# Sharing a causal attention block over four cores by contiguous pieces, with a program branch per piece

## The chip, the cores and the metric

One Trainium2 chip (trn2), one program on its 8 cores. Cores 0 to 3 form one die and work on the first sequence of the batch, cores 4 to 7 the other die and the second sequence. The metric is device time in microseconds (us) of the slowest core. Executions come in two states: in the fast one all cores have a like granted clock; in the slow one a die runs at a lower clock and is over 1% longer.

Engines in the profile: PE (matmul), PEld (its weight loads, beside PE), DVE (vector), ACT (activation functions), POOL, SP; the last two here mainly issue DMA.

## The reference, cut to what matters

```python
D_MODEL, BATCH, SEQ, N_META = 2048, 2, 4096, 16      # L = 4112 tokens per sequence
ATTN_HEADS, HEAD_DIM, D_FF = 8, 128, 8192

xn = rms_norm(h, norm_mix)
q, k, v, fg, cb, cc, cx, gl = split(xn @ w_in)        # 1024, 1024, 1024, 8, 3 x 1024, 4096 columns
q, k = rms_norm per head of 128
log_f = log_sigmoid(fg + b_fgate)                     # forget gate per token and head
s = q.k / sqrt(128) + cumsum(log_f)[query] - cumsum(log_f)[key];  s = -inf where key > query
a = softmax(s) @ v @ w_attn_out
c = (cb * causal_conv3(cc * cx)) @ w_conv_out
h = h + (sigmoid(gl_a) * a + sigmoid(gl_c) * c) @ w_o
h = h + relu(rms_norm(h, norm_mlp) @ w_up) ** 2 @ w_down
return h[:, N_META:]
```

Inputs and output are float32; both kernels multiply in bf16 with sums in float32. Causality is what the change is about: a query needs only keys before it, so late tokens cost more attention than early ones.

## The kernel before: the parts that the change touches

Every core ran the same instruction stream. Its own 1024 queries were every fourth 128-token block, so each core had to project K and V for all 4112 tokens, in groups of 512:

```python
groups = [(0, 1, NMETA)] + [(NMETA + 512 * g, 4, 128) for g in range(8)]
# ... per group g and head: one diagonal block of queries, then all later ones in threes
trips = [(gi - 1, 1, True)]
r = gi
while r < NR:                                     # NR = 8 query blocks
    n = min(3, NR - r)
    trips.append((r, n, False)); r += n
# ... exp, then a multiply by a mask that differs per core (data, not code)
S.op("act", lambda e: e.activation(out=PTf[:bt, pi, 0:W], in_=sbank[:bt, 0:W], func=AF.Exp,
                                   bias=bias_t[...], scale=SCALE), ...)
if diag:
    S.op("dve", lambda e: e.tensor_tensor(out=PTf[:, pi, 0:128], in0=PTf[:, pi, 0:128],
                                          in1=tri_bf[:, j, :], op=ALU.mult), ...)
```

x was squared on DVE for the token norm, and each head of K went through a norm of its own:

```python
S.op("dve", ... sq = stage * stage); S.op("dve", ... xg = stage * g_mix)          # per 128 rows of x
S.op("pe",  ... pb[sb_][:, :T] += ones_bf.T @ sq)                                 # 512-column sum
# head norm of Q and K: scale, square, 512-column sum, copy, Ln, Exp, final multiply
return [lambda: sA(0), lambda: sA(1), NOP, sB1, sB2, sC1, NOP, sC1b, sC2, sD]
```

Between attention and the rest stood a barrier and a second reading of the core's own x; weights were read straight from their matrices:

```python
S.barrier()
for t in range(2):
    rms_prep(xoT[:, TS[t]], 512, xog[:, :, TS[t]], ...)
# ... (cut)
src_ = dram[row0:row0 + kc * 128, col0:col0 + ncol].rearrange("(kc p) n -> p kc n", p=128)
S.dma("pool", view, src_, writes=keys)            # rows of ncol elements
```

## Time and profile before

The median of the first four runs was 2668.22 us (2665.5 to 2671.61).

The prediction below shows the spans of the cores, the head of the page, its slices, the stretches and PE's waits. One more view matters, the page's list of DMA queues; the queue that carries the weights (packets, MB, share of the 16 DMA engines over the span):

```profile
q0 software_dynamic: 324304, 125.87, 42.0%
```

### The profile page before, as it was taken

The page shows a single profiled execution, that of the slowest core. Times are in us where ns is not written, and L with a number is a line of the kernel's source. Part 1 is how long each engine was busy: PE and PEld are TensorE (multiplying, and loading weights), DVE is VectorE, ACT ScalarE, POOL GpSimd, SP SyncE. Part 2 cuts the span into 40 slices and gives each one's busy share as a digit, 9 for nine tenths or more (in the row PEclk, how much of TensorE's full clock was granted, in tenths as well). Part 3 has the DMA queues.
Part 4 walks back from the last instruction along what each step waited for, and adds up shares of the span by engine and source line. Part 5 has one row for each costly group of instructions (what it writes and reads, how often), then busy time and mean ns, then how long its engine had stood idle before and what let it go on. Part 6 is the DMA issues. An engine that isn't in the chain of part 4 may idle for free.

```text
span 2666.8 us, 36382 instructions; the slowest of 8 cores (2652.6 to 2666.8 us)
## 1 busy us (share of the span) xinstructions
PE 2419.1 (91%) x12522; PEld 1172.0 (44%) x12742; DVE 1027.7 (39%) x2170; ACT 586.9 (22%) x1198; POOL 189.8 (7%) x177
## 2 busy tenths in 40 slices
PE   5678889898988988389999999999999999999999
PEld 1234455554544445034444444444444444444444
DVE  5655546545465455335423233332111211211211
ACT  0312345444443334300011111121001101100100
POOL 1000000000000000111111121000000000000000
PEclk9868889898987968589999999999999999999999
DMA  9930101202022010967578778975566656666662
GB/s 199 127 88 11 54 19 46 64 1 64 1 64 64 1 40 1 184 78 74 58 69 79 72 71 94 162 100 74 76 79 80 79 71 74 77 80 79 78 118 90
DMA packets 366243, 196.12 MB, mean 74 GB/s; under 512 B 161136, under 2 KB 333168, under 8 KB 366064
## 3 DMA queue, kind: packets, MB, share of 16 engines
q0 software_dynamic: 324304, 125.87, 42.0%
q1 hardware_dynamic: 41760, 67.90, 8.8%
q8 instruction: 107, 1.75, 0.3%
q14 instruction: 72, 0.59, 0.1%
HBM read 311.22 MB, written 8.39 MB: 120 GB/s over the span
## 4 chain that ended last, share of the span: by engine, by line
PE 85%; DVE 6%; DMA 4%; issue 3%; ACT 1%; DVEq 0%; another core or an unknown queue 0%; SPq 0%; ACTq 0%
PE pc L875 16%; PE pc L894 16%; PE pb L339 10%; PE pb L434 8%; PE pc L759 6%; PE pc L807 4%; PE pc L805 4%; PE pc L837 4%; DMA stage<-xoT 3%; PE pb L584 3%; PE pb L559 3%; PE pc L803 2%; PE pc L801 2%; PE pb L313 1%; DVE xg L306 1%
## 5 line engine op out<-in xcount | busy, mean ns | idle before, releaser
L875 PE MATMUL pc<-xog,wring 128*128 128x512 bf16 x2008 | 440.6, 379 | 2.1
L894 PE MATMUL pc<-mT,wring 128*128 128x512 bf16 x2006 | 440.5, 379 | 2.2
L568 ACT ACTIVATE PT<-pb,small 128x128 bf16<-128x128 f32 (+4 forms) x664 | 276.4, 454 | 407.1 <-PE pb L559 209.2
L894 PEld LDWEIGHTS pc<-mT,wring 128*128 128x128 bf16 x2048 | 200.4, 98 | 241.6
L875 PEld LDWEIGHTS pc<-xog,wring 128*128 128x128 bf16 x2048 | 200.3, 98 | 241.5
L339 PE MATMUL pb<-xg,wk 128*128 128x512 bf16 (+1 forms) x1123 | 253.0, 369 | 2.6 <-issue 1.0
L434 PE MATMUL pb<-wv,xg 128*128 128x512 bf16 (+1 forms) x1028 | 245.1, 382 | 1.4
L882 ACT ACTIVATE mT<-tmp 128x512 bf16<-128x512 f32 x128 | 80.6, 629 | 691.2 <-DVE tmp L879 691.2
L559 PE MATMUL pb<-QT,KT 128*128 128x128 bf16 (+4 forms) x664 | 190.4, 298 | 46.4 <-ACT PT L568 39.1
L879 DVE SCALAR_TENSOR_TENSOR tmp<-pc,rstd_o 128x512 f32<-128x512 f32 x128 | 88.6, 692 | 355.0 <-PE pc L875 351.2
L898 DVE TENSOR_TENSOR h<-h,pc 128x512 f32<-128x512 f32 x128 | 88.1, 688 | 353.4 <-PE pc L894 353.4
L584 PE MATMUL pb<-Vg,PT 128*128 128x129 bf16 (+1 forms) x1216 | 190.8, 245 | 30.0 <-DVE PT L573 27.4
L759 PE MATMUL pc<-xog,wring 128*128 128x512 bf16 x752 | 166.7, 382 | 1.2 <-issue 0.2
L584 PEld LDWEIGHTS pb<-Vg,PT 128*128 128x128 bf16 (+1 forms) x1216 | 113.3, 108 | 112.4 <-issue 77.7
L112 POOL DMA_DIRECT2D wring<-w_in x56 | 64.3, 1159 | 1370.6 <-issue 964.7
L339 PEld LDWEIGHTS pb<-xg,wk 128*128 128x128 bf16 x1152 | 104.8, 102 | 108.6 <-issue 13.9
L434 PEld LDWEIGHTS pb<-wv,xg 128*128 128x128 bf16 (+1 forms) x1056 | 99.1, 98 | 102.4 <-issue 2.5
L600 DVE SCALAR_TENSOR_TENSOR acc<-acc,small,pb 128x387 f32<-128x387 f32 (+2 forms) x160 | 72.8, 455 | 174.5 <-PE pb L584 160.7
L313 PE MATMUL pb<-sq,ones_bf 128*128 128x512 bf16 (+1 forms) x162 | 82.0, 507 | 62.0 <-DVE sq L304 56.1
L814 DVE TENSOR_TENSOR tmpA<-pc,rstd_o 128x512 f32<-128x512 f32 x64 | 41.3, 686 | 212.1 <-PE pc L807 212.1
L304 DVE TENSOR_TENSOR sq<-stage 128x512 bf16<-128x512 f32 (+1 forms) x176 | 112.7, 640 | 23.4 <-DMA stage<-xoT 11.2
L837 PE MATMUL pc<-mT,wring 128*128 128x512 bf16 x501 | 114.8, 379 | 1.0 <-DVE mT L822 0.5
(116 smaller groups left out, 2135.0 us busy)
## 6 DMA issues: line engine op xcount, KB each, us to landing
stage<-xT SPq DMA_DIRECT2D x128, 256.0 KB, 3.3
wring<-w_up POOLq DMA_DIRECT2D x32, 1024.0 KB, 11.1
wring<-w_down POOLq DMA_DIRECT2D x32, 1024.0 KB, 8.9
wring<-w_in POOLq DMA_DIRECT2D x56, 512.0 KB, 8.8
stage<-xoT SPq DMA_DIRECT2D x96, 256.0 KB, 8.1
wv<-w_in POOLq DMA_DIRECT2D x8, 1024.0 KB, 18.2
wring<-w_o POOLq DMA_DIRECT2D x8, 1024.0 KB, 13.3
yT<-h SPq DMA_DIRECT2D x32, 256.0 KB, 2.0
```

The lines of the kernel that those rows point to most:

```text
L304: S.op("dve", lambda e: e.tensor_tensor(out=sq[:, qi, :T], in0=stage[:, si, :T], in1=stage[:, si, :T], op=ALU.mult), reads=[sk], writes=[qk])
L313: S.op("pe", lambda e: e.matmul(pb[sb_][:, :T], lhsT=ones_bf[:], rhs=sq[:, qi, :T], start=(kc == 0), stop=(kc == KC - 1)), reads=[qk, "one ...
L339: ins = e.matmul(bank[:, :T], lhsT=wbuf[:, kc, h * 128:(h + 1) * 128], rhs=xg[:, kc, :T], start=(kc == 0), stop=(kc == KC - 1))
L434: ins = e.matmul(bank[:bt, :], lhsT=xg[:, kc, j * bt:(j + 1) * bt], rhs=wv[:, kc, ch * 512:(ch + 1) * 512], start=(kc == 0), stop=(kc == K ...
L559: S.op("pe", lambda e: e.matmul(sbank[:bt, 0:W], lhsT=KT[:, h, j * bt:(j + 1) * bt], rhs=QT[:, h, r0 * 128:r0 * 128 + W], start=True, stop ...
L568: S.op("act", lambda e: e.activation(out=PTf[:bt, pi, 0:W], in_=sbank[:bt, 0:W], func=AF.Exp, bias=bias_t[:bt, j * 8 + h:j * 8 + h + 1], s ...
L584: ins = e.matmul(obank[:, k * 129:(k + 1) * 129], lhsT=PTf[:bt, pi, k * 128:(k + 1) * 128], rhs=Vg[:bt, j, h, :], start=(j == 0 and k == 0 ...
L759: ins = e.matmul(bank[:, :], lhsT=w[:, kc, cs], rhs=xog[:, kc, TS[t]], start=(kc == 0), stop=(kc == KC - 1))
L805: ins = e.matmul(pc[b0 + 2][:, :], lhsT=wg0[:, kc, cs], rhs=xog[:, kc, TS[t]], start=(kc == 0), stop=(kc == KC - 1))
L837: ins = e.matmul(pc[bank][:, :], lhsT=wo[:, kc, cs], rhs=mT[:, kc, TS[t]], start=(kc == 0), stop=(kc == KC - 1))
L875: ins = e.matmul(pc[bank][:, :], lhsT=wu[:, kc, cs], rhs=hng[:, kc, TS[t]], start=(kc == 0), stop=(kc == KC - 1))
L894: ins = e.matmul(pc[bank][:, :], lhsT=wd[:, kc, cs], rhs=uT[:, kc, TS[t]], start=(kc == 0), stop=(kc == KC - 1))
```

## The change

The intent: do no arithmetic that causality makes useless, and keep PE fed. Core p of a sequence owns one contiguous piece. The pieces are cut so that the sum of matmul columns is about equal: the late ones have fewer tokens, since they do more attention. As the cores now do different things, the program holds four bodies and each core jumps to its own. With it come smaller changes: x stays on chip (no barrier, no re-reading), K is not normalised but its scale is given to exp, the diagonal mask is added by a matmul, the token squares of earlier tokens are made on ACT with an accumulated sum, and weights are laid out in memory as the tiles that are loaded. The core of a diff of 2303 lines, cuts marked:

```diff
+CUTS = [0, 1200, 2246, 3226, L]
+class Geo:
+    def __init__(self, p):
+        self.A, self.B = CUTS[p], CUTS[p + 1]
+        ...
+        self.et = [(max(0, self.A - 128 * (i + 1)), self.A - 128 * i) for i in range(nt)]   # earlier tokens
+        self.egroups = [list(range(g, min(g + 2, nt))) for g in range(0, nt, 2)]             # 256 at a time
 ...
+    cid = nc.values_load(T["cid"][0:1, 0:1], ...)
+    for p in nc.Switch(engines=engines, index=[cid] * 5, n=4):
+        emit(nc, sems, T, ps, Geo(p))
 ...  K: copy, square, one-column sums per tile of 128 keys; the scale goes into exp
+                S.op("dve", lambda e: e.tensor_copy(out=KT[ks][:, 0:N], in_=ps[st["b"]][:, 0:N]), ...)
+                S.op("dve", lambda e: e.tensor_tensor(out=sqk[sq][:, 0:N], in0=KT..., in1=KT..., op=ALU.mult), ...)
+                    for j, m, off in tiles:
+                        ins = e.matmul(ps[7][:m, col:col + 1], lhsT=sqk[st["q"]][:, off:off + m], rhs=on_h[:, 0:1], ...)
 ...
-                                out=PTf[...], in_=sbank[:bt, 0:W], func=AF.Exp, bias=bias_t[...], scale=SCALE),
-                                if diag: ... tensor_tensor(..., in1=tri_bf[:, j, :], op=ALU.mult)
+                            if diag:
+                                ins = e.matmul(ps[sb][:m, 0:mq], lhsT=id_bf[:, :m], rhs=mask_bf[:, off:off + mq], start=False, stop=True)
+                        S.op("act", lambda e: e.activation(out=PT[pt][:m, 0:N], in_=ps[st["s"]][:m, 0:N], func=AF.Exp,
+                                                           bias=small[:m, bcol:bcol + 1], scale=small[:m, kcol:kcol + 1]), ...)
 ...  token squares of earlier tokens, from a row-major copy of x
+                S.op("act", lambda e: e.activation(out=stage[i][:m, 0:1024], in_=stage[i][:m, 0:1024], func=AF.Square,
+                                                   accum_out=small[:m, col:col + 1]), ...)
 ...  attention steps and the next group's projections laid into one another by their cost
+        th = attn_thunks(units)            # steps of one group, values matmul 3 and accumulation 4 steps after the scores
+        merge(th, fill)                    # fill: V and K of the next group; in the last group some of the convolution
-        S.barrier()
-        ... rms_prep(xoT[:, TS[t]], 512, xog[:, :, TS[t]], ...)
+        S.dma("pool", ringv[i][:, :], T["wB"][k], writes=[("ring", i)])    # one 128 x 2048 tile, ring of eight
```

## The prediction

> **What bounds the kernel now.** I read the list of cores first, because a change that shares the work out anew is decided by the slowest core. The eight spans lie within 14.2 us (2652.6 to 2666.8) at granted clocks of 0.924 to 0.927, so today every core does the same work and none is disturbed. Next the head of the page and its slices:
>
> ```profile
> span 2666.8 us, 36382 instructions; the slowest of 8 cores (2652.6 to 2666.8 us)
> PE 2419.1 (91%) x12522; PEld 1172.0 (44%) x12742; DVE 1027.7 (39%) x2170; ACT 586.9 (22%) x1198; POOL 189.8 (7%) x177
> PE   5678889898988988389999999999999999999999
> PEclk9868889898987968589999999999999999999999
> ```
>
> PE is busy 91%, but the slices show two kernels: up to slice 16 PE has holes and a clock below full; after that it is full at full clock. I cut the span at the barrier and at the changes of source line (table of stretches; columns: us, busy us and instructions per engine, clock, DMA share, GB/s):
>
> ```profile
> 0.00:110.00 110.00, 69.36 (x255) 26.69 (x261) 66.49 (x117) 18.68 (x27) 13.04 (x15) 0.95 1.14 169
> 110.00:232.00 122.00, 94.06 (x523) 41.47 (x529) 68.65 (x168) 30.34 (x62) 2.28 (x2) 0.79 0.39 74
> 232.00:1064.00 832.00, 725.10 (x4544) 405.60 (x4609) 450.86 (x1140) 348.35 (x794) 0.00 (x0) 0.85 0.12 35
> 1064.00:1150.00 86.00, 27.78 (x112) 9.39 (x115) 28.79 (x75) 31.68 (x70) 11.42 (x10) 0.50 1.13 175
> 1784.00:2666.00 882.00, 875.30 (x3994) 398.53 (x4073) 175.94 (x255) 80.50 (x128) 67.34 (x59) 1.00 0.59 81
> ```
>
> Stage A (0 to 1064 us) is Q, then K and V of all 4112 tokens with attention. The next 86 us re-read x behind a barrier at half clock. Stage B (1150 to 2667) is convolution, gates, output projection and MLP: in its last 882 us, 4073 weight loads, so 216.5 ns per 512-column matmul. Stage B is nothing but streamed columns. Where stage A loses time, PE's waits say:
>
> ```profile
> PE pb L313 <- DVE sq L304: 56.1, 60, 8.3
> PE pc L217 <- ACT sq L215: 50.6, 43, 4.8
> PE pb L559 <- ACT PT L568: 39.1, 29, 4.6
> PE pb L584 <- DVE PT L573: 27.4, 42, 2.0
> PE pb L357 <- DVE scr L362: 19.5, 21, 2.9
> ```
>
> The token sums of squares wait for squaring (first, and second for the re-read), the scores for exp, the values matmul for the mask multiply on DVE, the head norms for a copy. One K/V period shows it as well: 650 to 716 us has PE 64.47 of 66 us at clock 1.00; 716 to 760 only 30.98 of 44 at 0.70, while DVE is busy 4.0 of 4.0 us in pieces of it, preparing the next x. So DVE and ordering bound the seams of stage A, PE everything else.
>
> **What the Trainium skill says.** "TensorE: Matmul & The Clock Gate", section "Wait — 56ns, not 53.3ns?": a warm matmul costs N/2.4 ns plus about 2.5. That gives 215.8 for N=512; the trace's 216.5 agrees. The same page's Part 1 (the HAM clock gate) says an idle window of about 3.4 us halves the clock; the 0.50 in the re-read and the 0.70 at the seams agree. It also warns of a 13/16 clock once three cores of a die run dense matmuls; this trace does not show it (1.00 through the MLP on all-core load), so I budget full clock. "DMA: Bandwidth & Descriptors", "Why small descriptors are slow": fixed cost per packet. The weight queue here moved 125.87 MB in 324304 packets, 388 bytes each, at 42% of the engines.
>
> **The change part by part.** I count columns streamed through PE and price them at N/2.4 + 2.5 ns.
>
> *Before.* Stage A: Q 131k columns, x and head norms 123k, K 526k, V 541k, scores 156k, values 157k: 1.634M, 681 us. Stage B with the re-read: 3.572M, 1488 us. Together 2169 us; 2667 were taken. The 498 us above it are 31 of 2.5 ns per matmul (12742 loads), 79 of the re-read (86 less 7 of columns), 19 at stage B's boundaries, and 369 of stage A's seams, small matmuls and half clock (1064 - 681 - 14).
>
> *Removed arithmetic.* Before, a core owned every fourth block, so it projected K and V for the whole sequence and swept masked blocks: 36 x 4 pairs and a meta block per head. Now core p of a batch owns one contiguous piece (cuts 0, 1200, 2246, 3226, 4112) and runs its own branch of the program: it projects K and V only for tokens up to its end, and touches only pairs on or below the diagonal. Pairs per head become 55, 135, 180, 210. The cuts give the late pieces fewer own tokens (n = 1184, 1046, 980, 886), so stage B shrinks or grows with n/1024. Per core, in us at 2.4 columns per ns:
> stage A 257, 430, 567, 684; stage B 1713, 1513, 1418, 1282; sums 1970, 1943, 1985, 1966. With 2.5 ns per matmul (p0: about 12500 matmuls, 31 us; p2 and p3: some 12000 to 13400, 30 to 33; p1 14500, 36): 2001, 1979, 2015, 1999. The saving over 2169 + 31 is 185 us for the worst core, p2.
>
> *Removed overhead.* (1) The x tile stays on chip from Q to the merge, so the barrier and re-read (86 us, of which the 7 us of columns are counted) go: -79. (2) K needs no normalised copy: its per-token scale goes into exp's scale, and its sum of squares is a one-column matmul, so the 512-column norms, copy, Ln, Exp and final multiply per head go. (3) The diagonal mask is a 128-column matmul, in place of 256 multiplies of 222 ns (55.0 us of DVE on PE's path for 27.4). (4) Token squares of earlier tokens go to ACT with an accumulated sum, from a second row-major read of x. (5) The forget-gate sums use pairs of tiles, two fp32 matmuls per 256 keys in place of 14 per 512; with the row-scale ones these were 64 us of PE busy here. (2) to (5) are what should shrink the 369 us, and what replaces them is priced next.
>
> *Does another engine become the bound?* An early group of 256 keys on p2: PE 98k columns, 40.8 us, plus small matmuls, about 43. ACT: per tile and head exp of 384, 384 and 212 columns, 579 + 579 + about 430 ns by the rows measured here, times 16 is 25.4 us; squares about 4 x 1.1, small ones 3: 33 us. DVE: K copies and squares 6, V 4.5, accumulators 8 x 1.6 = 13, scaling x 4.3, small 2: 30 us. PE still bounds, but ACT is 77% full, so I take 5% of the 450 us of p2's mixed part as lost: +22.
>
> *Other terms.* Start: Q's first chunk needs 4.2 MB of weights and 4.0 MB of x. The trace moved 199 GB/s in its first slice: 41 us, 23 of them covered by PE work, then a gap of a few us before the second chunk: +22. First K after V: +4. Boundaries of the MLP quarters and of stages, as stage B had (1517 against 1499): +15. Output tail +2. Core p2: 2015 + 22 + 22 + 4 + 15 + 2 = 2080. Core p3 likewise 1999 + 29 + 43 = 2071. Core p0, whose small own attention is ACT-bound (224 exps of about 0.5 us = 112 against 100 of PE), about 2070.
>
> **The rivals.** *Balance fails.* The cuts equalise columns, not losses: if mixed attention loses 12% rather than 5%, p3 and p2 carry it (580 and 450 us of it) and the kernel ends at 2112 (15%: 2130), with p0 some 40 us earlier. For it: exp rows of 0.37 to 0.58 us and PE waiting 39.1 us for them; against: the stretch 650 to 716, where K/V filled PE to 98%. *Weight traffic becomes the bound.* Each core now streams 2048-column tiles at 16 x 886/2.4 = 5.9 us each, ring of eight; today 1 MB takes a share of 0.59 with a period of 13.8 us. Per tile that is 0.5 MB in 5.9 us, 85 GB/s against 81: share 0.62 at the old packets, less at larger ones. Hidden, I think; the output projection, with three residual buffers at 8.1 us landing and units of 2.4 to 3.4 us, could stall by 10 to 30 us. *Only the removed arithmetic counts:* if seams persist in other places, -185 gives about 2480. The new seams must be far worse than I see for that. *Power:* denser PE on every core could draw the lower clock the page warns of; 13/16 through p2's stage A would add 567 x 3/13 = 131 us, half of that ends at 2145.
>
> **Range and chances.** The rival losses are one-sided: 2080 with a tail to 2130; a start at faster DMA and better overlap gives 2040. Time 2080 us, 2035 to 2135 eight times in ten. For within 2% (above 2615) some 500 us of new loss would be needed. Faster 0.97, same 0.02, slower 0.01.
>
> **What would show it.** Cores: spans within about 2% of each other, p0 (cores 0 and 4) with a stage A near 350 us and p3 with one near 780. No stretch at clock 0.50 after the start; mean clock 0.97 or above. Rows for convolution, gates and MLP at N/2.4 + 2.5 ns of about 396, 350, 490 and 444 columns. PE waits for exp and DVE in the mixed part together below 60 us, and none for weights beyond the start. The prediction is wrong if PE in the attention part is busy under 90%, if one slice is over 3% longer than the rest, or if PE waits on weight tiles in the MLP.

## The result, and the profile after

The median of the ten timed runs is 2208.2 us (2150.87 to 2552.58), against 2668.43 us of before in the same rounds. Ratios in this text are the mean time of one kernel's fast runs over that of the other's of the same rounds, so not quite the ratio of medians: here 0.8069, with a 95% interval of 0.8059 to 0.8078. The direction was right, the size was not: 2080 us was predicted and 2135 us was the top of the range.

Two different things lie in the 2208. Five of the ten timed runs were slow, and their times reach from 2261.25 to 2552.58; the five fast ones lie between 2150.87 and 2155.15, and the median fell between the two sets (2155.15 and 2261.25). A slow run's record shows what that is. Cores 0 to 7 of the one of 2539.29 us, span and clock:

```
2535.3 2536.0 2523.1 2519.6 | 2127.2 2136.8 2142.4 2151.1
 0.811  0.811  0.822  0.822 |  0.992  0.990  0.992  0.990
```

One die lost nearly a fifth of its clock; the other one did its usual time. Of the 14 runs of before three were slow too (2837.67, 2923.95, 3066.34). So what follows is about the fast runs: some 2152 us, 72 more than predicted.

The list of cores (span, mean granted clock) of the profiled run, which was fast:

```profile
core 0: 2129.9 us, clock 0.993
...
core 5: 2145.2 us, clock 0.986
...
core 7: 2148.9 us, clock 0.990
```

The shortest core is 0.9% below the longest: four different programs end together, at almost full clock. The head of the page and its slices:

```profile
span 2148.9 us, 38630 instructions; the slowest of 8 cores (2129.9 to 2148.9 us)
PE 2066.8 (96%) x13886; PEld 1252.5 (58%) x13886; DVE 815.1 (38%) x1920; ACT 682.8 (32%) x1390; POOL 124.4 (6%) x245
PE   4799899999999998999999999999999999999999
PEclk9899999999999999999999999999999999999999
```

The holes and the clock of 5 to 8 tenths that the first sixteen slices of before had are gone but for the first slices. What is left I read from the table of stretches of core 7, the slowest (us; busy us and instructions of PE, PEld, DVE, ACT, POOL; clock; DMA share; GB/s):

```profile
10.00:50.00 40.00, 19.96 (x86) 8.75 (x87) 6.49 (x15) 7.81 (x8) 4.72 (x9) 0.96 1.01 204
50.00:116.00 66.00, 51.01 (x236) 25.51 (x235) 27.30 (x52) 36.77 (x61) 4.58 (x15) 0.87 0.81 169
116.00:167.00 51.00, 51.00 (x340) 34.95 (x339) 15.05 (x47) 0.00 (x0) 0.00 (x0) 0.97 0.28 50
167.00:290.00 123.00, 109.12 (x1141) 89.60 (x1139) 62.83 (x204) 74.38 (x179) 0.00 (x0) 0.97 0.18 54
290.00:805.00 515.00, 504.65 (x4918) 404.45 (x4919) 319.93 (x910) 393.25 (x844) 4.23 (x8) 1.00 0.33 98
805.00:863.00 58.00, 50.83 (x301) 25.14 (x299) 24.77 (x51) 26.44 (x52) 1.59 (x3) 0.91 0.30 57
...
1378.00:2148.00 770.00, 767.43 (x4097) 395.67 (x4096) 158.35 (x256) 76.58 (x133) 63.87 (x121) 1.00 0.53 93
```

A busy share does not tell how much was streamed, because a short matmul's record lasts longer than the gap to the next one (a one-column matmul's record is 165 ns). So I priced the matmuls of each stretch as the prediction did, N/2.4 + 2.5 ns for N columns, the one-column sums at 30 ns and the float32 sums at some 77 ns, as two experiments below give, and took this from the wall time (the stretch left out above, 863 to 1378 us, had PE busy for 512.84 of 515 us):

| core 7, us | wall | streamed | lost | the prediction's loss |
|---|---|---|---|---|
| 0 to 116: Q | 116 | 59 | 57 | 22 (start) |
| 116 to 167: own V | 51 | 49 | 2 | 0 |
| 167 to 290: own K, diagonal groups | 123 | 99 | 24 | 4 (first K) and 29 (5%) for these three |
| 290 to 805: earlier groups | 515 | 495 | 20 | |
| 805 to 863: last group | 58 | 37 | 21 | |
| 863 to 2149: convolution to MLP | 1286 | 1279 | 7 | 17 (boundaries, tail) |
| sum | 2149 | 2018 | 131 | 72 |

The prediction had 1999 streamed and 72 lost for this core, 2071 in all. PE's waits, to set beside those of before:

```profile
PE ps L520 <- DMA v_wq<-wqkv: 28.6, 5, 20.9
PE ps L943 <- ACT v_PT L958: 14.8, 23, 2.8
PE ps L547 <- ACT v_qsq L543: 11.4, 6, 3.3
PE ps L972 <- DVE v_acc L998: 9.3, 15, 2.5
```

The 50 to 56 us waits for squares are gone. Two of the sums of now lie in the start: Q's matmuls wait for Q's weights (28.6 us, of it 20.9 before the first), and the head norms' sums for a square (11.4). The waits for exp and for the accumulator (the two lines shown make 24 us) lie in the attention. Two pieces of the chain that ended last (start us, us, what), and the queue of the weights:

```profile
9.29 11.31 DMA v_wq<-wqkv
...
1474.18 95.89 PE ps L1319 x512
```

```profile
q0 software_dynamic: 33696, 125.94, 34.7%
```

The chain begins with a transfer of 11.31 us and its MLP is blocks of 512 matmuls in 95.9 us, 187.3 ns each at 442 and 444 columns; the priced 443/2.4 + 2.5 is 187.1. The weight queue moves the same bytes in a tenth of the packets (3738 bytes each).

The start in detail. The timeline of core 7 from 66 us (start us, us, engine, line, operation; in brackets the idle time before and what ended it). L547 is the sum of squares of one head on PE, L543 the square on ACT, L551 the Ln of the head norm, whose Exp follows it on ACT; between them DVE scales the next head out of its bank:

```profile
66.55 0.56 ACT L543 ACTIVATE v_qsq<-v_qraw 128x444 bf16<-128x444 f32 x1
...
67.25 0.35 PE L547 MATMUL ps<-v_qsq,v_on_h 128*128 128x444 bf16 x1 [3.32 <-ACT v_qsq L543]
...
67.80 0.63 ACT L551 ACTIVATE v_qrn<-ps,v_cst 128x444 f32<-128x444 f32 x1 [0.70 <-PE ps L547]
...
69.01 0.56 ACT L543 ACTIVATE v_qsq<-v_qraw 128x444 bf16<-128x444 f32 x1
```

From one ACT square to the next head's pass 2.46 us (66.55 to 69.01), and PE has one matmul of 0.35 us in it. Six heads of the first chunk of 444 tokens had been collected in six banks, so for a while there is nothing else for PE: it waits for a chain that goes round PE, ACT and DVE once per head.

### The profile page after: what moved, and what is told of

It is laid out like the page before. It is cut to its first block, busy times and chain, and to the rows that moved or that the text cites. A ratio compares the mean times of both kernels' runs of the same rounds, so it can differ in the third digit from the quotient of the medians.

```text
span 2148.9 us, 38630 instructions; the slowest of 8 cores (2129.9 to 2148.9 us)
## 1 busy us (share of the span) xinstructions
PE 2066.8 (96%) x13886; PEld 1252.5 (58%) x13886; DVE 815.1 (38%) x1920; ACT 682.8 (32%) x1390; POOL 124.4 (6%) x245
## 3 DMA queue, kind: packets, MB, share of 16 engines
q1 hardware_dynamic: 26784, 76.64, 11.5%
## 4 chain that ended last, share of the span: by engine, by line
PE 91%; ACT 3%; DMA 2%; issue 2%; DVE 1%; ACTq 0%; POOLq 0%; DVEq 0%; SPq 0%
PE ps L1299 18%; PE ps L1319 18%; PE ps L660 10%; PE ps L627 10%; PE ps L1204 9%; PE ps L1038 7%; PE ps L1255 4%; PE ps L972 4%; PE ps L943 4%; PE ps L1198 2%; PE ps L1200 2%; DMA v_wq<-wqkv 2%; PE ps L520 2%; ACT v_PT L958 1%; ACT v_stage L878 1%
## 5 line engine op out<-in xcount | busy, mean ns | idle before, releaser
L958 ACT ACTIVATE v_PT<-ps,v_small 128x118 bf16<-128x118 f32 (+4 forms) x752 | 400.8, 584 | 149.9 <-PE ps L943 90.7
L1319 PE MATMUL ps<-v_uT,v_ring 128*128 128x444 bf16 (+1 forms) x2048 | 384.2, 349 | 0.0
L1299 PE MATMUL ps<-v_hng,v_ring 128*128 128x444 bf16 (+1 forms) x2048 | 384.2, 349 | 0.0
L1319 PEld LDWEIGHTS ps<-v_uT,v_ring 128*128 128x128 bf16 x2048 | 197.9, 97 | 185.7
L1299 PEld LDWEIGHTS ps<-v_hng,v_ring 128*128 128x128 bf16 x2048 | 197.8, 97 | 185.7
L943 PE MATMUL ps<-v_QT,v_KT 128*128 128x118 bf16 (+4 forms) x752 | 207.0, 285 | 15.9 <-ACT v_PT L958 14.8
L627 PE MATMUL ps<-v_wv,v_xg 128*128 128x387 bf16 (+3 forms) x1248 | 209.5, 312 | 0.0
L660 PE MATMUL ps<-v_xg,v_wk 128*128 128x256 bf16 (+1 forms) x1664 | 208.4, 269 | 0.0
L972 PE MATMUL ps<-v_VB,v_PT 128*128 128x129 bf16 (+3 forms) x1536 | 185.0, 222 | 13.7 <-DVE v_acc L998 9.3
L1204 PE MATMUL ps<-v_xog,v_ring 128*128 128x442 bf16 (+1 forms) x1024 | 196.8, 350 | 0.0
```

What stands on the lines that cost most here:

```text
L627: ins = e.matmul(ps[b][:m, 0:nh * 129], lhsT=lhs(kc), rhs=wv[:, kc, h0 * 129:(h0 + nh) * 129], start=(kc == 0), stop=(kc == KC - 1))
L660: ins = e.matmul(ps[b][:, 0:N], lhsT=wk[:, kc, h * 128:(h + 1) * 128], rhs=cols(kc), start=(kc == 0), stop=(kc == KC - 1))
L943: ins = e.matmul(ps[sb][:m, 0:N], lhsT=KT[ks][:, koff:koff + m], rhs=QT[:, h, lo:hi], start=True, stop=not diag)
L958: S.op("act", lambda e: e.activation(out=PT[pt][:m, 0:N], in_=ps[st["s"]][:m, 0:N], func=AF.Exp, bias=small[:m, bcol:bcol + 1], scale=smal ...
L972: ins = e.matmul(ps[ob][:qh - ql, k * 129:(k + 1) * 129], lhsT=PT[pt][:m, ql - lo:qh - lo], rhs=Vt[vs][:m, h, :], start=(first and b == bl ...
L1204: ins = e.matmul(ps[b0 + 2 + g][:, 0:w], lhsT=wg[:, kc, :], rhs=xog[:, kc, lo:hi], start=(kc == 0), stop=(kc == KC - 1))
```

## The experiments

Each time is the median of the fast runs alone; each ratio is against the fast runs of before in the same rounds, which were four batches on different chips (medians of all runs of before in them, slow ones included: 2665.43, 2667.34, 2667.18 and 2667.45 us). The changed kernel's own ratio is 0.8069 (0.8059 to 0.8078); where the intervals overlap, a difference is not shown by the ratio. "V began" means the start of the first matmul that projects the values (V), in the one trace of a run. In the changed kernel and the seven other traces whose start is unchanged this was 115.6 to 118.4 us on core 7 and 133.0 to 135.0 on core 4, so a shift of 2 to 3 us is within the scatter.

### Equal pieces

```diff
-CUTS = [0, 1200, 2246, 3226, L]
+CUTS = [0, 1040, 2064, 3088, L]
```

> Right result: cuts at 1040, 2064, 3088, so every core owns 1024 tokens (and none is given less for its longer past). Columns then: 1703, 1869, 2034, 2198 us against 1970, 1943, 1985, 1966. If the cuts carry the balance: cores 3 and 7 take 2198 plus the 183 us that core 7 now has above its columns, so 2370 to 2400, cores 0 and 4 about 1870. Rival (late cores are bound by something other than columns): cores 3 and 7 stay under 2300.

2404.39 us, ratio 0.9015 (0.8989 to 0.9041). The list of cores:

```profile
core 4: 1852.1 us, clock 0.986
...
core 7: 2398.3 us, clock 0.987
```

The two cores between them took 2037.9 and 2217.2 us: three steps of about 180 us. The columns of these pieces, priced as in the prediction without its 2.5 ns, are 1703, 1869, 2034 and 2198 us, so each core lies 149 to 200 us above them. The counting of columns carries the balance: with equal pieces half of the change's gain would be gone. The mean over the cores is hardly changed by the cuts (2127 against 2141 us); the longest core is what they set.

### A quarter of the Q weights (wrong result)

```diff
-    for k2 in range(2, 8):
-        wq_dma(k2)
...
-   lhsT=wq[:, kc, h * 128:(h + 1) * 128]
+   lhsT=wq[:, kc % 4, h * 128:(h + 1) * 128]
```

> Wrong result on purpose: only the first quarter of the Q weights is loaded and used for all sixteen k-steps, so 3.1 of 4.2 MB (as bf16) leave the first load. Theory START-BYTES (the first 50 us are set by the bytes of weights and x): PE's waits for the Q weights fall from 28.6 us to about 11 (the first tile), the first chunk is done near 40 us instead of 57, and the whole kernel ends 10 to 17 us earlier (about 2137 against 2152). Rival START-CHAIN (what sets the end of the Q stage is the head-norm chain on ACT and the x of the second chunk): Q still ends near 110 to 116 us and the time falls by under 6 us.

2144.15 us, ratio 0.8037 (0.8018 to 0.8057). On core 7 the first matmul still waited for its weight tile until 23.1 us; V began at 110.2 us against 115.6 before this edit, on core 4 at 122.5 against 134.0. So three quarters of the bytes of Q's weights, 3 MB, were worth 5 us at that point on core 7, 11 on core 4, and 8 us in the end: between what the two theories expected. The first chunk ended some 7 us earlier, but the row of head norms stood behind it as before.

### Q's squares on DVE

```diff
-            S.op("act", lambda e: e.activation(out=qsq[st["s"]][:, 0:w], in_=qraw[st["r"]][:, 0:w], func=AF.Square),
+            S.op("dve", lambda e: e.tensor_tensor(out=qsq[st["s"]][:, 0:w], in0=qraw[st["r"]][:, 0:w], in1=qraw[st["r"]][:, 0:w], op=ALU.mult),
```

> Right result: the square of each Q head is made on DVE instead of ACT, so ACT's chain per head goes from square, Ln, Exp (1.8 us) to Ln, Exp (1.2 us), and ACT's x squares come sooner. START-CHAIN: PE's wait of 11.4 us for that square falls under 5 and the Q stage of the slowest core ends at about 105 us instead of 116: the kernel gains 6 to 11 us. START-BYTES: the x of the second chunk lands at the same time, and the gain is 0 to 3 us.

2150.7 us, ratio 0.8069 (0.8053 to 0.8084), no gain; V at 112.3 us on core 7, and at 127.9 against 134.0 on core 4. Most of the wait was renamed: PE's waits for the square (11.4 us) became 7.0 us for the Exp of the head norm. Taking one link out of a ring of three engines leaves the ring.

### More x loads in flight

```diff
+    NX, LA = 8, 7                      # eight staging buffers, seven loads ahead (were three ahead)
...
-    for k2 in range(3):
+    for k2 in range(LA):
         xp_load(0, k2)
```

> Right result: x comes through eight staging buffers, seven loads ahead, instead of three (the extra five lie where K's weights come later). Theory START-LATENCY (the second chunk's x comes late because only three loads of 0.45 MB are in flight, and its squares then hold up the first chunk's head norms in ACT's queue): the second chunk of Q starts some 10 to 20 us sooner, Q's last matmul on core 7 starts near 95 instead of 109, kernel 10 to 18 us faster. Rival START-CHAIN (the order of norms and x squares on ACT and PE sets it, not the landing of x): gain under 5 us. START-BYTES: gain near 0, first tile of weights later by up to 5 us.

2156.85 us, ratio 0.8088 (0.8064 to 0.8111). The second chunk's x was on chip by about 65 us, and Q ended no earlier: V began at 117.5 us on core 7. PE's waits in its first 125 us show that the same time was given another name, x in place of weights:

```profile
PE ps L526 <- DVE v_xog L491: 28.4, 5, 22.4
PE ps L553 <- ACT v_qsq L549: 10.5, 6, 2.5
```

The latency of x was not what held the start. It also shows how little the name of a wait says while the DMA engines are full.

### The next chunk's heads laid between the norms

```diff
-    q_items = q0_items[:2] + [q_item(6, 0)] + q0_items[2:4] + [q_item(7, 0)] + q0_items[4:]
+    q1 = [q_item(h, 1) for h in range(8)]
+    q_items = q0_items[:2] + [q_item(6, 0), q0_items[2], q_item(7, 0), q0_items[3], q1[0], q0_items[4], q1[1], q0_items[5]] + q1[2:]
...
```

(with the two edits before it)

> Right result: as the deep-x run, and the heads of the second chunk are interleaved with the last heads of the first, so that PE has 3-us blocks of work while the first chunk's head norms go round ACT, DVE and PE; Q's squares are on DVE. START-CHAIN (between 57 and 84 us PE waits in order for six head norms at 2.45 us each, with two heads of work of its own): Q's last matmul on core 7 starts at 92 to 100 us instead of 109 to 111 and the kernel gains 8 to 18 us, about 2140. Rival (the x of the second chunk is not ready, or the weights of V land too late): under 4 us.

Fast runs of 2145.65, 2147.69 and 2170.42 us (two of five were slow), ratio 0.8092 (0.8028 to 0.8155): by the ratio alone this is open, since one fast run has one core of the second die at 2169.0 us with a clock of 0.972. In the profiled run all cores but one are earlier than in the changed kernel (core 5 is 1.1 us later); on core 7 V began at 108.4 us against 115.6, on core 4 at 124.9 against 134.0. The three edits together are worth 7 to 9 us there, of which the squares on DVE alone gave 3 and 6; the expectation had 8 to 18 for the kernel. What the interleaving gives without them was not run.

### Both together: interleaved, with a quarter of the Q weights (wrong)

> Wrong on purpose: the interleaved start of the earlier run with only a quarter of the Q weights loaded and used. Core 7's values began at 115.6 us in the changed kernel, at 110.2 with a quarter of the weights, at 108.4 with the interleaving. If the bytes and the chain of the head norms are two costs that add up: values begin at 102 to 105 and the fast runs take 2136 to 2142. If they stand in for each other (each hides the other): the two together begin below 99 and take under 2136. If the interleaving had its gain from the same wait as the bytes: 107 to 110 and 2142 to 2148.

2133.48 us, ratio 0.8006 (0.7993 to 0.802). V on core 7 in the changed kernel and here (PE's matmuls of V; first and last start in us):

```profile
L627 PE MATMUL ps<-v_wv,v_xog x336: 271/328/533, 115.6 to 166.5; 128*128 128x387 bf16 x96, 128*128 128x258 bf16 x48, 128*118 128x387 bf16 x16, 128*118 128x258 bf16 x8
...
L631 PE MATMUL ps<-v_wv,v_xog x336: 271/328/532, 96.6 to 148.6; 128*128 128x387 bf16 x96, 128*128 128x258 bf16 x48, 128*118 128x387 bf16 x16, 128*118 128x258 bf16 x8
```

That is 19 us earlier, against 5.4 and 7.2 for the two kernels before that have one part each. Read alone, it looks as if bytes and norms hid one another, as the expectation put it for a start below 99. The other cores do not bear this out. On core 4 V began at 134.0 us in the changed kernel and at 122.5, 124.9 and 113.1 in the three: 11.5 and 9.1 alone, 20.9 together. In the means of the fast runs core 7 ended 8.3, 8.6 and 18.3 us earlier. So the two costs roughly add up, and that they hide one another is not shown. With both, 19 of the 57 us lost in the start of core 7 are accounted for. The largest of PE's waits in the start of this core (first 125 us):

```profile
PE ps L524 <- DMA v_wq<-wqkv: 19.7, 1, 19.7
```

The others are at most 3.6 us for each line. One large wait is left, the first: 19.7 us until the first weight tile is there. No DMA is issued before about 6 us on core 7 (in the changed kernel 3.3 us on cores 0 and 4, 6.1 to 6.9 on the others; 1.1 us on every core in the kernel before). Loading the core's number and jumping is what stands there in the program; the trace has no record of these instructions.

### Half of the squares of earlier tokens

```diff
-        loads = ... [("t", t, hf) for t in range(len(tl)) for hf in range(2)]
+        loads = ... [("t", t, hf) for t in range(len(tl)) for hf in range(1)]
```

(the missing half is replaced by the first one's sum; the result stayed within tolerance)

> Wrong result on purpose: of each earlier token's row only the first half is loaded and squared (the sum is doubled), which takes 26 of 52 squares of 1.24 us (32 us) off ACT on cores 3 and 7. Theory MIXED-ACT (attention with K and V loses because exp on ACT, 73% busy there, comes late): idle and loss of the mixed stretch (167 to 857 us, 50 us above its matmuls) fall by 10 to 20 us, kernel about 2137. Rival MIXED-LATENCY (waits come from the order and the few score, output and P buffers, not from how full ACT is): change under 4 us.

2151.02 us, ratio 0.8087 (0.805 to 0.8125): no gain. In the earlier groups (290 to 805 us) PE was busy 504.74 us in place of 504.65. In one place it shows. In the changed kernel, where the first earlier group is prepared beside the diagonal groups, its squares stand in ACT's queue before exps, and they wait for their DMA:

```profile
259.28 1.06 ACT L878 ACTIVATE v_stage<-v_stage 128x1024 f32<-128x1024 f32 x1 [1.43 <-DMA v_stage<-xr]
...
261.49 0.21 PE L943 MATMUL ps<-v_QT,v_KT 128*128 128x118 bf16 x1 [1.68 <-ACT v_PT L958]
```

L878 is the square, L943 the scores matmul that waits for a bank whose exp (L958) stands behind it. With half the squares PE was busy 4.18 of the 6 us from 257 to 263 (2.52 before), and the clock stayed at 1.00 in the 6 us after it (0.50 before). The loss from 167 to 280 us fell from 21 to 16 us in this one trace, but the span only by 1.5 us, as some 1.5 us more were lost before V was done and 2 us after 280 us: within the scatter of traces. So the squares are seen to hold PE up in this place; that they cost the kernel anything is not shown.

### One step more between scores, values and accumulation

```diff
-    def attn_thunks(units, offs=(0, 0, 3, 4)):
+    def attn_thunks(units, offs=(0, 0, 4, 5)):
```

> Right result: the values matmul runs four units behind its scores instead of three (accumulation five instead of four). MIXED-LATENCY: PE's waits for exp (14.8 us) and for the accumulators (11.6 us) fall by half, gain 5 to 12 us. MIXED-ACT: the three score banks still hold PE to exp's pace, gain under 3 us; a loss of up to 10 us is possible as all five P buffers are then in use.

2153.24 us, ratio 0.8075 (0.8056 to 0.8095), no gain; the waits of the scores for exp 16.8 in place of 14.8 us, those for the accumulators 9.0 in place of 11.6. One step more of distance does not win back what is lost. In the earlier groups there was little to win: PE was busy for 504.65 of 515 us in the changed kernel.

### More convolution in the last group

```diff
-            share = max(0.0, sum(0.62 for _ in units) - sum(u[0] for u in units))
+            share = max(0.0, sum(1.0 for _ in units) - sum(u[0] for u in units))
+            fill.append((0.2 * share, NOP[1]))
...
-        tstep = max(1, (len(units) // 2 - 2) // 8)
+        tstep = max(1, (len(units) // 2 - 2) // 8) if i + 1 < NG else 1
```

With the larger share alone, undefined values were read in the bank that K's sums and the convolution share, so the convolution starts later here and the tail of K comes first.

> More convolution matmuls are laid between the steps of the last attention group (which has no projection of a next group to fill PE with), and the tail of the last K is moved to the front of it. On core 7 that group is the stretch 805 to 863 us, where 58 us passed for some 37 us of streamed columns: 21 us lost. Theory LAST-GROUP (PE has too little to do there and waits for exp and for the accumulator): the loss falls to 5 to 12 us, and cores 3 and 7 end 8 to 16 us earlier, near 2135; fast runs 2138 to 2146, since cores 1, 2, 5 and 6 gain as well. Rival ENGINES (ACT and DVE set the pace of the last group, PE's filler only moves): the end of attention moves by what conv is done in it, and the span stays within 4 us.

2151.38 us, ratio 0.8078 (0.8052 to 0.8103): no gain. The stretches show why (core 7, same columns as above; first two of the changed kernel, then those with this edit):

```profile
819.00:830.00 11.00, 7.93 (x46) 3.82 (x45) 5.45 (x11) 5.80 (x15) 0.00 (x0) 0.84 0.00 0
...
841.00:852.00 11.00, 8.56 (x40) 3.71 (x39) 4.55 (x8) 4.64 (x8) 0.53 (x1) 0.74 0.28 50
```

```profile
819.00:830.00 11.00, 10.08 (x60) 4.77 (x58) 5.71 (x11) 3.62 (x7) 0.27 (x1) 1.00 0.00 0
...
841.00:852.00 11.00, 11.00 (x67) 5.68 (x65) 4.46 (x8) 3.30 (x6) 0.00 (x0) 1.00 0.32 49
...
870.00:900.00 30.00, 27.58 (x158) 14.45 (x156) 15.51 (x40) 2.27 (x5) 1.58 (x3) 1.00 0.45 78
```

PE is fuller here and its clock higher, so the loss between 805 and 863 us fell from 21 to 13 us. But PE now waits from 870 to 900 us, where the changed kernel had 30.00 of 30 busy: the last scores come after 863 us, and 6 us of loss came up behind it. Filler shifted the loss and took little of it away (21 us became 13 and 6), as the rival expects. That ACT and DVE set the pace of the last group is what the rival says; no run shows it.

### Doubled sums of squares of K

```diff
-                    for j, m, off in tiles:
+                    for j, m, off in tiles + tiles:
```

> Right result: every one-column matmul of K's sums of squares is done twice (248 more on cores 3 and 7, 72 to 170 on the others). My prediction's sum left these out. Theory UNCOUNTED (in the mixed part PE is full, so small matmuls count in full[...]): cores 3 and 7 grow by 13 to 16 us, cores 0 and 4 by about 4; kernel about 2167. Rival HIDDEN (PE waits for ACT and DVE there anyway): growth under 5 us.

2160.0 us, ratio 0.8101 (0.8082 to 0.8119), slower than the changed kernel. In the profiled run core 7 took 2156.4 us, 7.5 more for 248 further matmuls: 30 ns each on the path. In the means of the fast runs it is 7.0 on core 7 and 8.3 on core 3. The expectation had 13 to 16 us.

### Doubled float32 sums of the forget gates

```diff
                 e.matmul(ps[7][:, 0:nt8], lhsT=LN_f, rhs=sp, start=True, stop=True)
+                e.matmul(ps[7][:, 16:16 + nt8], lhsT=NO_f, rhs=sp, start=True, stop=True)
+                e.matmul(ps[7][:, 0:nt8], lhsT=LN_f, rhs=sp, start=True, stop=True)
                 return e.matmul(ps[7][:, 16:16 + nt8], lhsT=NO_f, rhs=sp, start=True, stop=True)
```

> Right result: the two fp32 matmuls per earlier group that sum the forget gates are done twice. UNCOUNTED: 26 more instructions pairs on core 7, at the 0.22 to 0.26 us of their rows, so 6 to 12 us on cores 3 and 7, 0 on cores 0 and 4. Rival HIDDEN, or cheap like the one-column matmuls (30 ns each): under 3 us.

2155.08 us, ratio 0.8079 (0.8062 to 0.8097): by the ratio no difference is shown. In the profiled run core 7 took 2153.3 us, 4 more for 52 further matmuls, 77 ns each; in the means of the fast runs cores 3 and 7 took 3 more, and cores 0 and 4, which have no earlier tokens, took no more. The expectation had 6 to 12 us.

### The re-reading put back

```diff
+    for e in ENGS:                       # wait for every engine and every DMA, as the old barrier did
+        for t in allk: S._wait(e, t)
+    for c in range(nch):                 # load, scale, square and sum the own x once more
+        ...
     merge(conv[conv_used:], c0_thunks())
```

> Right result: after attention all engines meet at a barrier and the own x is loaded, scaled, squared and summed again, as the kernel before did. My prediction priced what this removes at 79 us for 1024 tokens, so for 886 to 1184 tokens here 60 to 90 us: kernel about 2230. Rival (it would be hidden behind convolution work): under 20 us, which a barrier rules out; or only the transfer time, 7.3 MB at 200 to 300 GB/s, 25 to 40 us.

2194.2 and 2195.17 us, ratio 0.8229 (0.8211 to 0.8247). The spans are 2175.4 to 2193.7 us, in the mean of the eight cores 43 us longer than those of the changed kernel. The prediction had booked 79 us for it, the expectation 60 to 90, the rival 25 to 40: it lies between. The re-reading put back here is the changed kernel's own loader (its packets, its 886 to 1184 tokens), not the old one, so what the old one's 86 us were made of beyond this is not settled.

### Weights of the MLP read from the untiled matrices

```diff
-        S.dma("pool", ringv[i][:, :], T["wB"][k], writes=[("ring", i)])
...                                      # other tiles as before; for the MLP's tiles:
+            src = T[w][r0:r0 + 2048, c0:c0 + 128].rearrange("(k p) n -> p k n", p=128)
...
```

> Right result: the MLP's weight tiles are read from the untouched matrices, 128 columns wide (512-byte pieces, as the kernel before did in its gates stretch at 78 GB/s and share 0.78), instead of from the tiled copy that the host lays out. HIDDEN TRAFFIC: share goes from 0.53 to about 0.9 at the 88 to 93 GB/s needed, PE does not wait, time within 5 us. Rival WEIGHTS-BOUND: cores 3 and 7, with 6.0 us per tile the fastest, wait in the MLP and grow by 20 to 100 us while cores 0 and 4 (8.0 us per tile) do not.

2156.12 us, ratio 0.8082 (0.8064 to 0.8101): no difference shown. The MLP's stretch of core 7:

```profile
1378.00:2148.00 770.00, 768.47 (x4104) 396.19 (x4103) 159.19 (x258) 77.95 (x135) 138.19 (x121) 1.00 0.98 93
```

The DMA share went from 0.53 to 0.98 at the same 93 GB/s, PE's busy time did not move. The layout is worth almost nothing in time here, but it took the DMA engines from almost full to half full. "DMA: Bandwidth & Descriptors", section "Why small descriptors are slow (HBM only)", in the Trainium skill names a fixed cost per packet as the reason; the trace agrees in direction (254 bytes per packet here, 3641 in the changed kernel, for like bytes in this stretch). The edit also makes the reads strided, and no run separates the two.

### The gains put together

The interleaved start, the fuller last group, and new cuts, since in the interleaved run cores 0 and 4 ended some 20 us before cores 3 and 7:

```diff
-CUTS = [0, 1200, 2246, 3226, L]
-WMAX = 1200
+CUTS = [0, 1206, 2252, 3230, L]
+WMAX = 1208
```

> The interleaved start of the earlier run, the fuller last group of the run beside this one, and cuts 1206, 2252, 3230. If all three gains are real and add up: cores 0 and 4 near 2134 (2123 to 2128 with the cuts before, and some 1.75 us per token), cores 3 and 7 near 2125 to 2133 (2142, less 7 for four tokens, less the last group's gain); fast runs 2135 to 2143, ratio near 0.802. If the last group gives nothing: 2138 to 2146.

Fast runs 2137.55, 2138.0, 2141.82 and 2144.85 us, ratio 0.8029 (0.8016 to 0.8042); its interval lies below that of the changed kernel (0.8059 to 0.8078). It beats both kernels, by about 12 us over the changed one (means of the fast runs). The spans lie between 2128.3 and 2136.6 us, so the balance is now within 0.4%. Four tokens fewer were to give cores 3 and 7 about 7 us, and they end 7 and 8 us earlier than in the interleaved run, so nothing is left over for the fuller last group.

## Why the prediction was right or wrong, point by point

**The step that failed** is the size of two terms, in a sum whose other parts held. "Start: ... +22" measured 57 us before V, since PE also waits before the bytes begin and after they have landed. "5% of the ... mixed part" with "First K after V: +4", 33 us for this core, measured 65, nearly all of the excess at the two ends of that part. Streamed work was 20 us more, the boundaries 10 less. That this last miss took away some of the others is luck. The parts follow, in the order of the prediction where that is possible.

**What bounds the kernel: right.** PE's busy share went from 91 to 96% and the mean clock from 0.92 to 0.99; DVE, ACT and POOL are at most 38% busy over the span. In the earlier groups of core 7 ACT is busy for 393.25 of 515 us, 76%, close to the 77% that was worked out for p2.

**Balance from columns: right.** The eight spans lie within 0.9%, and the equal cuts moved each core by about what its columns say. The slowest core was a p3 (2148.9) and not p2 as predicted (2142.6). The "about 2070" for p0 is not the sum of the terms given for it (2001 + 43 + 12 = 2056).

**Price of a streamed column: right**, to 0.2 ns in the MLP (187.3 against 187.1).

**"Boundaries ... +15" and "Output tail +2": too much.** 7 us were lost from 863 us on: -10 for core 7.

**The sum of streamed work, "1999": 20 us too little.** The prediction said that what replaces the removed sums "is priced next", but the one-column sums and the float32 sums got no term of their own; doubling them measured some 7.5 and 4 us (the second within the noise of the ratio). About 3 us more are columns: those of the trace of core 7 make 1969 us at 2.4 per ns, the prediction had 1966. The rest is not split.

**"Start: ... +22": the largest mistake.** 57 us were lost before V instead of 22, and 2 more in V. The prediction counted bytes (41 us at 199 GB/s, 23 covered), and the trace agrees with that part: at 204 GB/s the DMA engines are full from 10 to 50 us. It left out what lies before and behind the bytes: a first issue at 6 us where the kernel before had one at 1.1; a first tile that needs 11.3 us; and, after the bytes, "a gap of a few us", which is six head norms of about 2.5 us each with little else for PE to do. The edits on bytes and order together took away 19 us of V's start time on core 7; much of the rest stands before the first matmul, at 20.9 us.

**"I take 5% of the ... mixed part as lost" and "First K after V: +4": right for the middle, missing at its ends.** In the long stretch of equal groups 20 of 515 us were lost (4%). In the diagonal groups before it 24 of 123, in the last group 21 of 58. The 5% had been set from one steady group of 256 keys and was carried over to ends with another mix. What was lost there is only partly explained. ACT's queue with squares that wait for DMA is seen in one place of one trace, some 5 us; for the last group the runs only show that more work for PE does not help. In the stretches above PE is idle for 14 of the 123 us and 7 of the 58, and the clock of 0.91 in the last group is worth some 5 us more (0.09 of 58, an estimate). That is where time went and not why: the cause of the other 40 us of the two ends is open.

One cost of this part was also too small. The prediction took an exp of 384 columns at 579 ns, from the old kernel, where its scale was a constant. In the new one the scale comes from a tile, one value per key, and the same shape takes 669 ns (ACT's lines by form, before and after):

```profile
L568 ACT ACTIVATE PT<-pb,small 128x384 bf16<-128x384 f32 x224 | 121.5, 579 | 147.8 <-PE pb L584 75.2 <-PE pb L559 68.4 <-DVE sq L304 2.6
...
L958 ACT ACTIVATE v_PT<-ps,v_small 128x384 bf16<-128x384 f32 x440 | 284.4, 669 | 98.0 <-PE ps L943 62.3 <-PE ps L972 29.0 <-PE ps L679 5.5
```

At 128 columns it is 455 ns (core 4) where it was 366, about the same 90 more. For the 752 exps of core 7 that is an estimated 68 us of ACT's time. Whether PE pays for it in the diagonal groups and the last group is a rival that no run tested, and neither did one isolate the scale as the reason; an exp with a constant scale would do both.

**The sum for core 7:** streamed +20 (2018 less 1999, rounded up), start and V +37, mixed part +32, boundaries -10: 79, and 2149 less 2071 is 78.

**"-79" for the re-read: too much as booked, without effect on the total.** It measured 43 us. The total was added up from new terms, and the 79 stood only in the account of the old kernel.

**The rivals.** "Balance fails" was wrong in the form given, since p0 lost nearly as much (core 4: 2132 us for 2011 streamed, 55 of the 121 lost before V), but its premise, mixed attention that loses 12% and not 5%, was nearer: 65 of 696 us is 9%. "Weight traffic becomes the bound" is refuted for the MLP even with small packets, and in the output projection and the norm behind it PE's waits are 2.1 us in all, none of them for a residual. "Only the removed arithmetic counts" (2480) is refuted. The lower clock of "Power" came in a part of the runs (0.81 in two of them) and not in the fast ones: it was given as a cost of stage A, and it came as a state of a whole die. That power causes it is not shown, and three of 14 runs of the kernel before were slow too.

**The range.** It reckoned with the fast state alone, and had 2.6% of room upward, 55 us, for a sum of small terms that were mostly estimated low; the fast runs needed 72. The checks that the prediction named mostly passed: balance, rows, no waits for weights in the MLP, mean clock, waits in the mixed part below 60 us (about 30). Three failed: a stretch at clock 0.50 after the start (263 to 269 us), and the end of attention, at 855 us on core 7 where 780 was given and at 381 on core 4 where it was 350. None of its three signs of being wrong came on the slowest core: PE is busy 91% of the time up to 855 us, the spans agree, and no weight tile is waited for in the MLP. So the signs looked for lost balance and lost PE time on a scale that the miss did not reach. The sum of waits was too mild a check as well: it names about 30 of the 65 us that the mixed part lost.

## What to carry to other kernels

Count streamed columns to set the cuts and trust them; but give the start and each change of stage a term of its own, taken from a drawn order of what waits for what, and not a percentage from a steady stretch. When an instruction changes its form, measure its new cost before carrying the old one over (exp: 579 to 669 ns). When two causes are tried alone and together, compare several cores before concluding that they hide each other: core 7 suggested it (5 and 7 us against 19), core 4 shows them adding up (11.5 and 9.1 against 20.9). And a quiet layout change can be worth nothing in time and still halve the load of the DMA engines.

## What the Trainium skill lacked or had wrong

- "TensorE: Matmul & The Clock Gate", Part 1, tells to budget 13/16 of the clock for sustained dense matmul on all cores. Here fast runs with eight cores of dense matmuls held 0.985 to 0.993 in the mean and 1.00 through the MLP; only two slow runs had a die at 0.81 to 0.82 (lowest 0.808), about 13/16, and then the whole die, as the page says, but not the other one; the other slow runs had a die between 0.84 and 0.94. Of the 13 executions of the changed kernel 6 were slow.
- The same page, section "Back-to-back issue gap", says that in a real stream of weight loads and matmuls N/2.4 + 2.5 over-counts at N=512 (about 131 ns) and under-counts at N=128 (about 81 ns). Here 4096 pairs of weight load and matmul at 442 and 444 columns came at 187.3 ns, which is the formula (187.1), and eight K matmuls of 118 columns took 0.58 us with a last record of 0.21, so 53 ns each, where the formula has 52. Its floor of about 25 ns for small N is near the 30 ns that 248 further one-column matmuls took.
- No page gives what a program pays that first loads its core's number and jumps to one of four bodies: "Advanced Engine Details and Errata", section "Control Flow Timing", has the branch instruction alone (51 to 108 ns), and "Runtime: NRT & Kernel Launch" names an instruction fetch after a far branch without a time for it. Here the first DMA was issued 2.2 to 5.8 us later than in the kernel without it (3.3 us for the first case, 6.1 to 6.9 for the later ones, 1.1 before); load, jump and fetch were not separated.
- The start-up of a full DMA system was not to be had from "DMA: Bandwidth & Descriptors": the first 512 KB weight tile took 11.31 us from issue to landing beside the loads of x (204 GB/s over all queues from 10 to 50 us), where tiles of the same size in the MLP took 5.3 us.
